# Two groups of recurrences beside the input projection: all tokens' recurrence columns first, split tokens kept in DRAM, RWKV in three groups of PSUM banks, RG-LRU in halves

## The chip, the core and the metric

The kernel runs on one core of a Trainium2 chip. The metric is the device time of one execution in microseconds, as the median of several runs. A core has five engines with their own instruction streams: TensorE (PE: matmuls, with a separate queue of weight loads, PEld), VectorE (DVE), ScalarE (ACT), GpSimd (POOL) and SyncE (SP), which here issues nearly all DMA transfers. Each stream is executed in order. An instruction that needs another engine's result waits, and everything behind it on its engine waits with it.

## The reference

One layer of a hybrid trunk over T = 2048 + 16 tokens of width 1024. The input projection's columns are shared out over three groups of heads; their outputs are joined, projected, and followed by a gated feed-forward network.

```python
p = rms_norm(h, norm_mix_pre[l]) @ w_in[l]
pa = p[..., :A_COLS]
pb = p[..., A_COLS:A_COLS + B_COLS]
pc = p[..., A_COLS + B_COLS:]
oa = rg_lru_group(xa, ya, ...)
ob = forgetting_attention_group(q, k, v, f_logit, ...)
oc, v_own = rwkv7_group(pc, ...)
mixed = jnp.concatenate([oa, ob, oc], axis=-1) @ w_out[l]
h = h + rms_norm(mixed, norm_mix_post[l])
f = causal_dwconv(rms_norm(h, norm_ffn_pre[l]) @ ffn_up[l], ffn_conv[l])
gate, val = jnp.split(f, 2, axis=-1)
f = (jax.nn.gelu(gate, approximate=True) * val) @ ffn_down[l]
h = h + rms_norm(f, norm_ffn_post[l])
```

RG-LRU (256 channels, columns "a", 512 of them) and RWKV-7 (4 heads of 64, columns "c", 1024 of them) are recurrences over the tokens:

```python
_, h = lax.associative_scan(combine, (a, b), axis=1)
...
s_kk = jnp.einsum('bhij,bhj->bhi', S, kk_t)
S = S * w_t[:, :, None, :] - s_kk[..., None] * (kk_t * a_t)[:, :, None, :] + v_t[..., None] * k_t[:, :, None, :]
```

The attention (8 heads of 64, columns q, k, v of 512 each and 8 gate columns) is causal softmax attention with a cumulated forget gate added to the scores.

## The kernel before

All products are float32-like: each operand is split into a high and a low part (`wh`, `wl` of the weights, `xh`, `xl` of the tokens), and `mm3` (L168 to L170) adds three matmuls of the parts.

**Input projection** (`w_in_norm`, `w_in_part`, `w_in_step`). The tokens come in three parts of two blocks each (400 + 384, 384 + 384, 256 + 256 columns). For each part, `w_in_norm` loads, normalises, transposes (tile `pst`) and splits the tokens into `xh` and `xl` in SBUF. Then 24 units of 128 output columns run, in the order c (8 units), a (4), k (4), v (4), q (4); a unit loads 128 columns of `w_in` (tile `raw`, 512 KB), splits them (ACT L162, DVE L163) and makes 8 x 3 matmuls into a bank `psp` for each block. ACT or DVE copies the bank to a staging tile (`stp`, `sth`, `stl`), and SP stores that to DRAM (`scr_p`, `scr_kh`, `scr_kl` and so on). Everything behind the projection reads from DRAM. `psp` has a pool of five PSUM banks; the staging tiles have two slots (`sth`) and one (`stl`, `stv`).

**Recurrences** (`recurrences`, `lru_block`, `Rwkv.block`, `Rwkv.chunks`). They go over nine blocks of four chunks of 64 tokens (the last has one chunk), three blocks for each part of the projection. `lru_block` works on both halves of its 256 channels at once, in buffers that it shares with RWKV (`rwk`, `rwr`, `rwsq`, `rwe`). `Rwkv.block` makes the operands, `chunks` solves a triangular system for each chunk: diagonal blocks go through DRAM (`da`, `rwia`, `dx`, `rwxu`), 15 steps alternate between POOL (L1119) and DVE (L1120), small matmuls follow. Up to the mark `SOLVED` a block is its front; the rest is kept as `R.ending` and put behind the front of the next block. RWKV uses two banks `rps` and one `eps`.

**What sets the order.** The program text runs the projection's units and, through `Beside`, lets the recurrences make `PACE` = 1.5 steps for each unit, once 14 units of the part are out. The framework then schedules all instructions of the program over the engines: each engine's stream is a fixed list that it makes, with an instruction placed where its operands and buffers are planned to be ready. So recurrence rows stand between projection rows on PE, and those that don't fit reach into attention, although the text ends the recurrences first.

**Beside and behind it.** `weight_sums` makes the differences of `ffn_down` (tile `ds`) that the last stage needs: loads, four POOL subtractions for each of ten pairs of rows, stores; its text runs beside the projection. Attention (`Attn.run`) goes over the 8 heads for the first 1024 tokens (score tiles `sc`, maxima `mx`, values `po`; ACT makes the exponentials `p` at L658), then over the 8 heads for the rest, with the output projection (`pswo`) beside it. FFN-up (`ffn_up`, tile `psu`) has three super-blocks of 22 units; in the first one POOL also makes the sums and differences of its weights (`uq`, L1626), DVE and POOL split the operands (`uw`, L1554). FFN-down is tile `psd`.

## Time and profile before

| | us |
|---|---|
| median of 3 runs | 3112.99 (3111.31 to 3129.72) |
| span of the profiled execution | 3106.3 |
| PE busy in the span | 2921.8 (94%) |
| weight load busy | 2493.4 (80%) |
| DVE busy | 2208.1 (71%) |
| ACT busy | 1463.2 (47%) |
| POOL busy | 1318.1 (42%) |

The page gives the profiled execution's span, from its first to its last instruction, and not its total. A matmul's record overlaps with the next one's, since matmuls are pipelined, so PE's busy time is not PE at its peak; the distance from one start to the next is what a matmul takes from the engine. The granted clock is TensorE's, as a share of full speed. By the page's chain of waits, 61% of the span is PE, 14% DVE, 12% DMA.

```profile
PE   6998999999978999999989899999999999999998
PEld 6987988998855664565558899999999999787876
DVE  6248655676688788777745899897778777557766
...
PEclk9999999999977799999999999999999999999999
```

Each column is a fortieth of the span, 78 us. The weight load and the clock fall in the twelfth to fifteenth column, which is where the projection has ended and attention has begun.

### The profile page before, as it was taken

The page shows a single profiled execution, that of the slowest core. Times are in us where ns is not written, and L with a number is a line of the kernel's source. Part 1 is how long each engine was busy: PE and PEld are TensorE (multiplying, and loading weights), DVE is VectorE, ACT ScalarE, POOL GpSimd, SP SyncE. Part 2 cuts the span into 40 slices and gives each one's busy share as a digit, 9 for nine tenths or more (in the row PEclk, how much of TensorE's full clock was granted, in tenths as well). Part 3 has the DMA queues.
Part 4 walks back from the last instruction along what each step waited for, and adds up shares of the span by engine and source line. Part 5 has one row for each costly group of instructions (what it writes and reads, how often), then busy time and mean ns, then how long its engine had stood idle before and what let it go on. Part 6 is the DMA issues. An engine that isn't in the chain of part 4 may idle for free.

```text
span 3106.3 us, 52286 instructions
## 1 busy us (share of the span) xinstructions
PE 2921.8 (94%) x18488; PEld 2493.4 (80%) x18488; DVE 2208.1 (71%) x4322; ACT 1463.2 (47%) x2770; POOL 1318.1 (42%) x1436
## 2 busy tenths in 40 slices
PE   6998999999978999999989899999999999999998
PEld 6987988998855664565558899999999999787876
DVE  6248655676688788777745899897778777557766
ACT  4135334344534444445544555566666665324333
POOL 3310101101133465446743568743533334556665
PEclk9999999999977799999999999999999999999999
DMA  6664333353352334444336455565555565535444
GB/s 202 231 205 142 103 89 107 106 150 98 96 139 65 77 90 128 118 125 107 80 101 199 155 180 167 171 197 169 165 168 163 167 188 160 180 102 173 143 166 143
DMA packets 456502, 443.71 MB, mean 143 GB/s; under 512 B 82496, under 2 KB 373514, under 8 KB 453408
## 3 DMA queue, kind: packets, MB, share of 16 engines
q1 hardware_dynamic: 455856, 439.99, 47.8%
q8 instruction: 145, 2.38, 0.3%
q14 instruction: 117, 0.96, 0.1%
q0 software_dynamic: 384, 0.39, 0.0%
HBM read 314.39 MB, written 125.87 MB: 142 GB/s over the span
## 4 chain that ended last, share of the span: by engine, by line
PE 61%; DVE 14%; DMA 12%; POOL 5%; issue 4%; ACT 3%; SPq 0%; POOLq 0%; DVEq 0%; ACTq 0%
PE psu L168 7%; PE psu L169 7%; PE psu L170 7%; PE psp L168 4%; PE psp L169 4%; PE psp L170 4%; PE po L676 3%; PE psd L170 2%; PE psd L168 2%; PE psd L169 2%; DVE uw L1554 2%; PE mx L527 2%; DVE uy L1665 2%; PE sc L653 2%; PE pswo L170 2%
## 5 line engine op out<-in xcount | busy, mean ns | idle before, releaser
L168 PE MATMUL psu<-xo,uw 128*128 128x344 f32 x1848 | 592.1, 324 | 23.5 <-DVE vb L1709 12.5
L169 PE MATMUL psu<-xo,uw 128*128 128x344 f32 x1848 | 594.5, 322 | 0.0
L170 PE MATMUL psu<-xo,uw 128*128 128x344 f32 x1848 | 584.3, 321 | 0.0
L168 PE MATMUL psp<-xh,wh 128*128 128x384 f32 (+2 forms) x1152 | 380.6, 330 | 0.0
L170 PE MATMUL psp<-xh,wl 128*128 128x384 f32 (+2 forms) x1152 | 377.6, 328 | 3.0 <-DVE wl L163 3.0
L169 PE MATMUL psp<-xl,wh 128*128 128x384 f32 (+2 forms) x1152 | 376.7, 327 | 0.0
L168 PEld LDWEIGHTS psu<-xo,uw 128*128 128x128 f32 x1848 | 348.6, 189 | 28.8 <-DVE vb L1709 15.5
L1554 DVE TENSOR_TENSOR uw<-uq,uw 128x512 fp32r<-128x512 f32 x352 | 333.6, 954 | 53.3 <-ACT uw L1553 49.9
L169 PEld LDWEIGHTS psu<-xo,uw 128*128 128x128 f32 x1848 | 349.8, 189 | 0.0
L170 PEld LDWEIGHTS psu<-xo,uw 128*128 128x128 f32 x1848 | 348.1, 189 | 0.0
L1553 ACT ACTIVATE uw<-uq 128x512 fp32r<-128x512 f32 x462 | 286.9, 627 | 90.9 <-PE psu L170 43.2
L658 ACT ACTIVATE p<-sc,bias 128x512 f32<-128x512 f32 (+4 forms) x352 | 197.5, 591 | 218.9 <-PE sc L654 184.1
L1665 DVE SCALAR_TENSOR_TENSOR uy<-psu,ffn_cols,uy 128x342 f32<-128x342 f32 (+1 forms) x396 | 223.7, 567 | 70.5 <-ACT uy L1663 69.6
L697 POOL TENSOR_TENSOR acc<-acc,p 128x512 f32<-128x512 f32 (+3 forms) x208 | 228.5, 1102 | 84.2 <-DVE acc L697 36.5
L1671 POOL TENSOR_TENSOR uy<-uy,uy 128x342 f32<-128x342 f32 (+1 forms) x132 | 145.8, 1105 | 225.4 <-DVE uy L1665 88.9
L170 PEld LDWEIGHTS psp<-xh,wl 128*128 128x128 f32 x1152 | 218.9, 190 | 10.4 <-issue 5.5
L168 PEld LDWEIGHTS psp<-xh,wh 128*128 128x128 f32 x1152 | 218.8, 190 | 7.1 <-issue 4.7
L169 PEld LDWEIGHTS psp<-xl,wh 128*128 128x128 f32 x1152 | 218.7, 190 | 6.7 <-issue 4.3
L1554 POOL TENSOR_TENSOR uw<-uq,uw 128x512 fp32r<-128x512 f32 x110 | 158.7, 1443 | 137.1 <-ACT uw L1553 116.7
L530 DVE TENSOR_REDUCE mc<-mx 128x1 f32<-128x400 f32 (+5 forms) x320 | 171.8, 554 | 57.5 <-PE mx L527 55.7
L1554 DVE TENSOR_TENSOR fo<-u,fo 128x896 fp32r<-128x896 f32 x88 | 106.4, 1209 | 122.3 <-ACT fo L1553 122.3
L1626 POOL TENSOR_TENSOR uq<-uq,uq 128x512 f32<-128x512 f32 x88 | 137.6, 1566 | 113.0 <-DMA uq<-in_ffn_up_dram 96.4
(460 smaller groups left out, 6539.2 us busy)
## 6 DMA issues: line engine op xcount, KB each, us to landing
uq<-in_ffn_up_dram SPq DMA_DIRECT2D x220, 256.0 KB
uq<-scr_us SPq DMA_DIRECT2D x176, 256.0 KB
raw<-in_w_in_dram SPq DMA_DIRECT2D x72, 512.0 KB
scr_us<-uq SPq DMA_DIRECT2D x88, 256.0 KB
u<-scr_ff SPq DMA_DIRECT2D x88, 256.0 KB
scr_ff<-uy SPq DMA_DIRECT2D x110, 171.0 KB
q<-scr_qh SPq DMA_DIRECT2D x96, 128.0 KB
ds<-in_ffn_down_dram SPq DMA_DIRECT2D x10, 1024.0 KB
```

Of the source, the lines that this page charges most:

```text
L168: nc.tensor.matmul(out, ah, bh, start=first, stop=False, skip_group_check=more)
L169: nc.tensor.matmul(out, ah, bl, start=False, stop=False, skip_group_check=more)
L170: nc.tensor.matmul(out, al, bh, start=False, stop=last, skip_group_check=more)
L530: self.reduced = nc.vector.tensor_reduce(mc[:rows, i, ci : ci + 1], ps[:rows, :full], axis=AX.X, op=ALU.max)
L658: last = nc.scalar.activation(p[:rows, :w], ps[:rows, :w], AF.Exp, bias=bias[:rows, j : j + 1])
L676: mm = nc.tensor.matmul(po[at : at + 64, c0:n], v1[:rows, j], p[:rows, : n - c0], start=start and i < 2, stop=end and i + 2 >= len(group), ...
L697: eng.tensor_tensor(a, ps_[0][0][:rows, c0:n] if start and i == 1 else a, p[:rows, : n - c0], op=ALU.add)
L1553: core.nc.scalar.activation(hi, src, AF.Copy)
L1554: (eng or core.nc.vector).tensor_tensor(lo, src, hi, op=ALU.subtract)
L1626: core.nc.gpsimd.tensor_tensor(raw[:], self.raw[x][:], self.raw[y][:], op=op)
L1665: stt(y[:, :n], src[:, i : n + i], cw[:, 44 * i + cc : 44 * i + cc + 1], y[:, :n], op0=ALU.mult, op1=ALU.add)
L1671: core.pooled = nc.gpsimd.tensor_tensor(v[:, :n], g[:, :n], v[:, :n], op=ALU.mult)
```

## The change

The projection is put in another order, and what lies beside it is fitted into other buffers:

- Four parts instead of three (528, 512, 512, 512 tokens); blocks of 272, 256 and three times 512 columns. The c and a columns of all parts come first, part by part, then k, v and q of parts 2, 3, 0 and 1. The buffers `xh`, `xl` are two sets that take turns, so the split tokens of parts 0 and 1 are stored in DRAM (`scr_xs`) and loaded again. There are 96 loads of weights, not 72.
- Recurrences of a part (two blocks each, three for the last) start when its c and a columns are out, at a pace of 3 steps for each unit. A block runs to its end before the next one's text begins; there is no `SOLVED` and no `ending`.
- PSUM: the projection has three banks, not five; RWKV has two for its solve (`rps`), two for making operands (`eps`) and one for its end (`ops`).
- RG-LRU works on one half of the channels at a time, in buffers of its own; its two halves are put between the steps of RWKV's block.
- Staging tiles of all kinds share three slots. The gate's small tiles move there too.
- The differences of `ffn_down` are made in halves of 256 columns, in FFN-up's text. Attention takes its second bank for maxima from another pool.

```diff
@@ def w_in_norm
+PARTS = 4
+W_IN_TILES = (0, 5, 9, 13, 17)
+W_IN_SPLIT = {0: 3}
...
+    for s, rows in () if kept else tiles:
+        src = meta if s < META else x[s - META : s - META + rows, :]
+        norm_transpose(core, pools, psum, src, rows, gain, [(hi, lo, s - t0, 0, rows)])
+    if part < 2:
+        for i, t in enumerate((hi, lo)):
+            flat = t[:].rearrange("p k t -> p (k t)").bitcast(F32)
+            place = scr["xs"][part, i, :, : KD * n]
+            core.nc.sync.dma_start(*((flat, place) if kept else (place, flat)))
@@ def w_in_step
-        oh = st.tile([P, 400], F32R, tag="sth", name=core.n("sth"))
-        ol = st.tile([P, 400], F32R, tag="stl", name=core.n("stl"), bufs=1)
+        oh = st.tile([P, 512], F32R, tag="sth", name=core.n("sth"))
+        ol = st.tile([P, 512], F32R, tag="sth", name=core.n("stl"))
@@ class WIn
+    def units(self, blocks, columns):
+
+        for kind, c0 in columns:
+            w = w_in_weights(self.core, self.pools, self.w_in, c0)
+            for block in blocks:
+                after = w_in_step(self.core, self.pools, self.psum, w, block, kind, c0, self.scr)
+                self.end()
+                self.waiting = after
+            yield
@@ class Rwkv
+    def po(self):
+
+        return self.epsum.tile([P, 512], F32, tag="ou", name=self.core.n("ops"), bufs=1)
+
     def pe(self):
 
-        return self.epsum.tile([P, 512], F32, tag="ae", name=self.core.n("eps"), bufs=1)
+        return self.epsum.tile([P, 512], F32, tag="ae", name=self.core.n("eps"), bufs=AE)
@@ def lru_block
+        u, r, g, al = (R.t([P, 256], "l" + s)[:, :n] for s in "urga")
...
-    stt(r, r, 1.0, al, op0=ALU.add, op1=ALU.mult)
-    stt(g, g, 1.0, u, op0=ALU.add, op1=ALU.mult)
-    yield
+        stt(r, r, 1.0, al, op0=ALU.add, op1=ALU.mult)
+        stt(g, g, 1.0, u, op0=ALU.add, op1=ALU.mult)
+        yield
@@ def weight_sums
+        for c in (0, 256):
+            t = pool.tile([P, 4, 256], F32, tag="us", name=core.n("ds"), bufs=1)
...
@@ def recurrences
-READY = 13
-PACE = 1.5
+PACE = 3.0
+AHEAD_UNITS = 4
+LRU_AFTER = 0, 1, 3, 4
...
+W_IN_RECUR = (0, 1), (2, 3), (4, 5), (6, 7, 8)
...
+    for b in W_IN_RECUR[part]:
+        lru = lru_block(R.core, R, scr, lk, b)
+        for i, _ in enumerate(R.block(b)):
+            if i in LRU_AFTER:
+                next(lru)
             yield
-        yield from R.ending
-        R.ending = gen
@@ def hybrid_block_kernel
-            ps_mm = pool(p1a, "ps_mm", 5, space=PSUM)
+            ps_mm = pool(p1a, "ps_mm", 5 - AE, space=PSUM)
...
+            for part in (1, 2):
+                units = ca(part)
+                emit(units, AHEAD_UNITS)
+                blocks.append(norm(part + 1))
+                emit(units)
+                gate(part)
+                recur(part)
+            emit(ca(3))
+            gate(3)
+            recur(3)
+            for part in (2, 3, 0, 1):
+                emit(kvq(part))
+                if part > 1:
+                    blocks[part - 2] = norm(part - 2, True)
...
+            if sup == 1 or j == NFF - 1:
+                next(more_sums, None)
```

(AE is 2.) PE's stream before, from the projection's last rows on: `eps` and `rps` are recurrence rows, `sc` and `mx` attention's.

```order
L170 MATMUL psp_9446<-xh_6168,wl_9235 128x256
L1032 MATMUL eps_8749<-rwix_8656,spr 128x256
L1032 MATMUL eps_8752<-rwix_8656,spr 128x256
L1052 MATMUL eps_8779<-rwsq_8649,bones 128x256
L653 MATMUL sc_10919<-q_1481_10828,k_1471_10801 128x512
L653 MATMUL sc_10925<-q_1481_10828,k_1471_10801 128x400
L527 MATMUL mx_10835<-k_1472_10802,q_1474_10806 128x144
L527 MATMUL mx_10840<-k_1472_10802,q_1474_10806 128x272
L527 MATMUL mx_10845<-k_1472_10802,q_1474_10806 128x400
L527 MATMUL mx_10850<-k_1472_10802,q_1474_10806 128x400
L527 MATMUL mx_10853<-k_1472_10802,q_1474_10806 128x128
L1284 MATMUL rps_8288<-ident,rww_895_6444 128x128 x2
```

Recurrence rows go on between attention's here for some 700 rows. PE's stream after, at the last recurrence rows (tile `ops`, of the ninth block):

```order
L168 MATMUL psp_9783<-xh_8502,wh_9746 128x256
L169 MATMUL psp_9783<-xl_8503,wh_9746 128x256
L170 MATMUL psp_9783<-xh_8502,wl_9747 128x256
L1296 MATMUL ops_8495<-ident,rwxu_8457 128x64
L1299 MATMUL ops_8495<-rwsg_8030,g_up 128x64
L168 MATMUL psp_9783<-xh_8502,wh_9746 128x256
L169 MATMUL psp_9783<-xl_8503,wh_9746 128x256
L170 MATMUL psp_9783<-xh_8502,wl_9747 128x256
```

All recurrence rows now stand between projection rows; 21 projection rows of 256 columns and 288 of 512 follow, and then attention's first rows without any recurrence row among them. The first RG-LRU matmul (`ga_w`) has 712 projection matmuls ahead of it before, and 672 now.

POOL's stream before, early in FFN-up's first super-block: `uq` are the sums of its weights, `uw` a split, `uy` products.

```order
L1554 TENSOR_TENSOR uw_17739<-uq_17706,uw_17739 128x512
L1626 TENSOR_TENSOR uq_17961<-uq_17924,uq_17926 128x512
L1626 TENSOR_TENSOR uq_17924<-uq_17922,uq_17924 128x512
L1626 TENSOR_TENSOR uq_17981<-uq_17961,uq_17922 128x512
L1626 TENSOR_TENSOR uq_18001<-uq_17928,uq_17981 128x512
L1554 TENSOR_TENSOR uw_17912<-uq_17767,uw_17912 128x512
L1626 TENSOR_TENSOR uq_18134<-uq_18097,uq_18099 128x512
L1626 TENSOR_TENSOR uq_18097<-uq_18095,uq_18097 128x512
L1671 TENSOR_TENSOR uy_17872<-uy_17849,uy_17872 128x342
```

Only the stage's own rows stand there, and its sums follow each other directly. POOL's stream after, at the same place, with the moved differences (`ds`):

```order
L1576 TENSOR_TENSOR ds_20879<-ds_20879 128x256
L1558 TENSOR_TENSOR uw_17419<-uq_17274,uw_17419 128x512
L1576 TENSOR_TENSOR ds_20879<-ds_20879 128x256 x2
L1632 TENSOR_TENSOR uq_17641<-uq_17604,uq_17606 128x512
L1576 TENSOR_TENSOR ds_20879<-ds_20879 128x256
L1632 TENSOR_TENSOR uq_17604<-uq_17602,uq_17604 128x512
L1677 TENSOR_TENSOR uy_17379<-uy_17356,uy_17379 128x342
L1632 TENSOR_TENSOR uq_17661<-uq_17641,uq_17602 128x512
L1632 TENSOR_TENSOR uq_17681<-uq_17608,uq_17661 128x512
```

The differences now stand between the sums, one or two at a time. All `ds` rows stand within this first super-block.

340 lines of the change are left out of this document (159 added, 181 removed).

## The prediction

> **What bounds the kernel now.** I read the busy time by stage first, then the share of single tiles in it, then the chain of waits. Columns of the windows: PE, PE weight load, VectorE (DVE), ScalarE (ACT), POOL busy, granted clock, DMA share, GB/s.
>
> ```profile
> 0.00:865.00 865.00, 810.58 (x6541) 746.30 (x6541) 522.58 (x1229) 355.31 (x634) 129.14 (x185) 0.98 0.46 138
> 1203.00:1700.00 497.00, 464.40 (x2017) 294.42 (x2018) 353.43 (x774) 238.79 (x444) 271.25 (x281) 0.98 0.46 127
> 1700.00:2640.00 940.00, 912.73 (x5703) 904.03 (x5701) 759.80 (x1145) 565.44 (x1121) 486.60 (x385) 0.99 0.56 169
> 2640.00:3106.00 466.00, 442.22 (x1866) 355.50 (x1866) 299.49 (x360) 164.60 (x273) 283.02 (x354) 0.97 0.45 151
> ...
> 50.00:150.00 100.00, 100.00 (x561) 100.00 (x560) 27.23 (x28) 23.94 (x32) 35.07 (x24) 1.00 0.66 220
> 200.00:865.00 665.00, 646.09 (x5672) 586.24 (x5670) 437.25 (x1010) 298.12 (x542) 59.56 (x116) 0.98 0.40 113
> 865.00:1203.00 338.00, 291.86 (x2364) 193.15 (x2363) 272.82 (x816) 139.07 (x299) 148.09 (x235) 0.79 0.38 92
> 1420.00:1560.00 140.00, 131.86 (x563) 70.22 (x562) 110.20 (x253) 77.39 (x133) 108.54 (x119) 0.99 0.38 90
> ```
>
> Every stage is near PE's limit but one. The projection (to 865 us) keeps PE busy for 810.6 of 865 us. The first half of attention (865 to 1203 us) does not: the weight load is busy for 193 of 338 us, the granted clock is 0.79, and DVE is at 272.8/338 = 0.81, the highest share of any of these stretches. What sits there beside attention are the last recurrences:
>
> ```profile
> L170 PE MATMUL psp<-xh,wl x1152: 274/337/702, 45.2 to 862.6; 128*128 128x384 f32 x95, 128*128 128x256 f32 x64, 128*128 128x400 f32 x33
> L653 PE MATMUL sc<-q,k x352: 170/392/974, 874.5 to 1591.6; 128*128 128x512 f32 x112, 128*128 128x272 f32 x16, 128*16 128x16 f32 x16, 128*128 128x400 f32 x16
> L1143 PE MATMUL rps<-rwxu,rwsc x792: 191/191/238, 367.6 to 1160.6; 32*32 32x32 f32 x198
> ```
>
> The projection's last matmul starts at 862.6, the first score at 874.5, and recurrence matmuls run to 1160.6. The first two windows below are those of the tile `rps`, the last two of `eps` (the recurrences' PSUM tiles): 205.5 us of their PE time lie in the projection, 126.3 us, at the low clock, beside attention.
>
> ```profile
> 0.00:865.00 865.00, 138.50 (x2560) 117.33 (x2560) 66.70 (x137) 33.66 (x67) 0.98 0.46 138
> 865.00:1203.00 338.00, 106.19 (x1602) 87.54 (x1602) 41.04 (x96) 21.35 (x44) 0.79 0.38 92
> ...
> 0.00:865.00 865.00, 66.99 (x219) 30.75 (x219) 22.45 (x58) 26.18 (x56) 0.98 0.46 138
> 865.00:1203.00 338.00, 20.12 (x63) 10.89 (x62) 7.39 (x18) 6.27 (x16) 0.79 0.38 92
> ```
>
> In the new order no recurrence row is left on PE behind the last projection row: the stage from 865 to 1203 loses them, the projection gets them. The sum is what the one saves less what the other pays.
>
> **Wider blocks: 4 us.** Starts of matmuls in a row, 400, 256 and 512 columns wide:
>
> ```profile
> 100.13 0.34 PE L168 MATMUL psp<-xh,wh 128*128 128x400 f32 x1
> ...
> 102.31 0.34 PE L168 MATMUL psp<-xh,wh 128*128 128x400 f32 x1
> ...
> 779.76 0.28 PE L169 MATMUL psp<-xl,wh 128*128 128x256 f32 x1
> ...
> 780.95 0.28 PE L170 MATMUL psp<-xh,wl 128*128 128x256 f32 x1
> ...
> 2699.44 0.39 PE L170 MATMUL psd<-qd,fo 128*128 128x512 f32 x1
> ...
> 2701.06 0.39 PE L168 MATMUL psd<-dw,fo 128*128 128x512 f32 x1
> ```
>
> 12 steps in 2.18 us, 10 in 1.19, 7 in 1.62: 182, 119 and 231 ns. A line through the last two is 7 ns + 0.4375 ns a column (400 give 182). Columns stay the same; matmuls fall from 3456 to 2880 (24 units x 24 x 5 blocks, not 6), 576 x 7 ns = 4 us. The Trainium skill, "TensorE: Matmul & The Clock Gate", section "Wait — 56ns, not 53.3ns?", puts the fixed part of a matmul at about 2.5 ns, which would make it 1.4 us; either way the width is no term that decides.
>
> **Start of the recurrences: 30 us earlier.**
>
> ```profile
> L1377 PEld LDWEIGHTS eps<-rwk,lru_ga_w x36: 186/189/331, 190.1 to 1011.0; 128*128 128x128 f32 x36
> L1018 DVE TENSOR_TENSOR_SCAN rwe<-rst,rwe x9: 403/1225/1457, 223.4 to 1037.5; 128x512 f32<-128x512 f32 x8, 128x128 f32<-128x128 f32 x1
> ```
>
> Ahead of the first RG-LRU matmul (190.1 us) PE had 712 projection matmuls of 400 and 384 columns (127 us by the line); now 672, of which 576 have 272 or 256 columns (93 us), and 16 transposes more (4 us). So about 160 us. The ffn_down differences that lay beside it leave too; I count no gain for that.
>
> **The stretch with recurrences: 745 us.** PE: 1899 projection matmuls lie between the first and the last recurrence row (288 of 272 columns, 267 of 256, 1344 of 512: 378 us). Gate and transposes there I take as half of the two rows below, 22 us, and 7 us for the v columns' transposes.
>
> ```profile
> L139 PE MATMUL pst<-ident,xt 128*128 128x128 f32 (+1 forms) x136 | 24.9, 346 | 25.1 <-DVE xt L126 17.0 <-DVE lruv L1336 7.7 <-DVE rs L90 0.4
> ...
> 0.00:865.00 865.00, 19.30 (x96) 17.47 (x96) 3.00 (x6) 2.70 (x6) 0.98 0.46 138
> ```
>
> The recurrences are 205.5 + 126.3 x 0.79 = 305 us. Sum 712 us; at the share of 200 to 865 us (646/665 = 0.97) 733 us. DVE: 522.6 us of the old stage; plus what the recurrences use of it after 865 us. That is 272.8 less attention's part: 118 steps there, against 109 in the stretch 1420 to 1560 with attention alone (110.2 us), so 119 us, and more for the shorter heads, of which 18 are prepared there against 8 (say 140 to 145). So 130 us. Plus 24 more weight splits at 1.26 us (30), plus RG-LRU in halves: ten operations of 512 become twenty of 256, 2 x 478 less some 740 ns, nine blocks, 19 us.
>
> ```profile
> L658 ACT ACTIVATE p<-sc,bias 128x512 f32<-128x512 f32 (+4 forms) x118 | 60.7, 544 | 82.0 <-PE sc L654 60.3 <-POOL acc L697 9.5 <-PE po L676 6.0
> ...
> L658 ACT ACTIVATE p<-sc,bias 128x512 f32<-128x512 f32 (+4 forms) x109 | 64.1, 619 | 54.1 <-PE sc L654 44.4 <-DVE acc L697 2.7 <-DVE rsv L90 2.4
> ...
> L556 DVE TENSOR_TENSOR q<-mx,ident 4x512 fp32r<-4x512 f32 x18 | 12.3, 682 | 3.2 <-PE mx L545 2.7
> ...
> L556 DVE TENSOR_TENSOR q<-mx,ident 4x512 fp32r<-4x512 f32 x8 | 5.5, 682 | 0.2
> ...
> L163 DVE TENSOR_TENSOR wl<-raw,wh 128x1024 fp32r<-128x1024 f32 x72 | 90.6, 1259 | 14.7 <-ACT wh L162 13.5 <-ACT rwsc L1106 0.9
> L1373 DVE SCALAR_TENSOR_TENSOR rwk<-rwraw,lru_cols,rwk x54: 270/478/631, 182.1 to 981.6; 128x256 f32<-128x256 f32 x42, 128x208 f32<-128x208 f32 x6, 128x64 f32<-128x64 f32 x6
> ```
>
> Together 702 us; off goes what lies ahead of the stretch (522.6 - 437.3 = 85) and behind it (70 us at the 0.27 of 50 to 150 us: 19): 598 us. At the highest share any long stretch shows, 0.81, that is 741 us. So both engines would be at the most they have shown here. I take 745; the ends are 712 (PE never waits) and 840: the blocks' scans stand (1037.5 - 223.4)/8 = 102 us apart, times 8.25 blocks.
>
> **The rest.** Behind the last recurrence row stand 288 matmuls of 512 and 21 of 256 columns: 69 us. The projection ends at 160 + 745 + 69 = 974. The first score follows 12 us later, as now. Then the 118 steps that took until 1203: alone a step took 140/109 = 1.28 us, so 152 us; scaled by DVE's work per step (142/118 against 110/109) 183. I take 174. The point that stood at 1203 comes at 974 + 12 + 174 = 1160: 43 us saved. DMA: 24 more weight loads, four stores and four reloads of the split tokens, all on SP; the reloads are issued one part (over 60 us) ahead of use, behind the stores they could hold up; hidden while the DMA share is 0.40, and at 0.66 (50 to 150 us) PE still was busy all the time. Cost 0.
>
> **ffn_down differences in FFN-up: 6 us lost.** The order puts all 80 halves between POOL's products of the first of three super-blocks (1720 to 2030 us; the second follows).
>
> ```profile
> 1720.00:2030.00 310.00, 289.71 (x1782) 286.06 (x1783) 273.99 (x369) 171.49 (x347) 226.48 (x158) 0.97 0.55 173
> 2030.00:2335.00 305.00, 304.80 (x1941) 303.74 (x1940) 238.68 (x379) 195.63 (x381) 130.17 (x108) 1.00 0.59 172
> ...
> L1572 POOL TENSOR_TENSOR ds<-ds 128x512 f32<-128x512 f32 x40 | 58.3, 1458 | 115.9 <-DMA ds<-in_ffn_down_dram 105.9 <-issue 7.6
> ...
> L1554 DVE TENSOR_TENSOR uw<-uq,uw 128x512 fp32r<-128x512 f32 x110 | 121.8, 1118 | 9.6 <-ACT uw L1553 9.4
> ...
> L1554 DVE TENSOR_TENSOR uw<-uq,uw 128x512 fp32r<-128x512 f32 x113 | 98.3, 875 | 20.0 <-ACT uw L1553 18.5
> ```
>
> POOL goes from 226 to 285 of 310 us: it fits. But the same DVE split takes 1118 ns where POOL is busy for 73%, 875 ns where for 43%; at 92% it gets some 150 ns longer, 17 us over 110, and DVE goes from 274 to 291 of 310. The slack covers it on average; 6 us for the times that it doesn't, 0 to 25 as ends.
>
> Sum: -43 + 6 = -37. The profiled execution has a span of 3106.3 us; its own total is not printed, but the median of the runs, 3113.0, lies 6.7 us above, which I take as what lies around it. 3113 - 37 = 3076 us.
>
> **Rivals.** (1) PE never waits and attention alone goes at its 152 us: 160 + 712 + 69 + 12 + 152 = 1105, 98 us saved, 3015. For it: PE reached 100% from 50 to 150 us. Against: DVE would be at 598/712 = 0.84, above all shown. 17%.
> (2) Banks. Projection tiles have three PSUM banks, not five, and all staging shares three slots. Evacuations wait for the stores of the tile before:
>
> ```profile
> ACT stp L56 <- DMA scr_p<-stp: 59.0, 9, 11.0
> DVE stp L58 <- DMA scr_p<-stp: 58.5, 8, 11.7
> ```
>
> Up to 11.7 us each, hidden today by four spare banks x 24 x 0.175 = 17 us; two spare ones give 11 us, and 6 with blocks of 256. If a quarter to half of the 117 us shows: 3076 + 30 to 59 = 3106 to 3135. 25%.
> (3) A lock. The Trainium skill, "SBUF — State Buffer", section "Who interferes with whom": a VectorE instruction with two SBUF inputs and a GpSimd one that reads SBUF exclude each other, whoever is second waits. The 1118 against 875 ns agree. As a mechanism here: the 58.3 us of differences block DVE for the share that such operations have of its time, at least 121.8/274 = 0.44, 26 us; DVE is at 300 of 310 us, its waits no longer fit, and some 20 us go to PE: 3076 - 6 + 20 = 3090. 10%.
> (4) Slower: the chain of one block. If a block can't follow the last in under the 102 us it takes now (dependent small steps, four trips through DRAM), the stretch is 840 us, PE waits for it in order, 95 us more: 3171. It decides from 745 + 37 = 782 us, or 95 us a block, on; a loss of 1% begins at 98.5. Against: these 102 us come from an order that alternated one block's end with the next one's start at a slower pace. 12%.
>
> **Numbers.** My forecast has 36%, its own range 3050 to 3100. 1% (31 us) is about what a measurement of this kernel can tell from no change. Faster: (1) and mine, 0.53; within 1%: (2) and (3), 0.35; slower: (4), 0.12. The range leaves out the lower half of (1) and most of (4): 3015 to 3140.
>
> **What would show it.** Last projection matmul near 974; first score 12 us later, no recurrence between; last recurrence some 70 us before; granted clock above 0.9 from there to the first w_out matmul; DVE near 0.81 in the stretch with recurrences; first super-block of FFN-up within 10 us of 310. Wrong, if projection evacuations wait for banks or slots with PE idle (2), or PE waits there for recurrence results (4).

## The result, and the profile after

The changed kernel takes 3144.85 us as the median of seven runs (3141.66 to 3152.1), the kernel before 3112.99 (3106.33 to 3133.18); the ratio is 1.0102 (1.0074 to 1.0130). The forecast was 3076 with a range that ended at 3140: the change makes the kernel 1% slower, and the forecast had it faster. The two profiled executions are 39.4 us apart, the medians 31.9, so stages are read to a few microseconds.

The page after has its slices 79 us wide:

```profile
PE   6889899999998888999998889999999999899998
PEld 5767777777896444565567788999999999787776
DVE  4477877776645677667746688797778777547667
...
PEclk9889799999999899999999899999999999999999
```

The dip of the clock that lay in the twelfth to fourteenth column before (7, 7, 7) is gone but for one 8. In its place the first columns have become poor (PE 6, 8, 8; clock 9, 8, 8, 9, 7), and the dip of PE where FFN-up's first super-block lies is wider: 8 in columns 22 to 24 (1651 to 1887 us), where the page before has 8, 9, 8 in columns 21 to 23. Marks of the stages, from the tiles of the changed kernel (first and last start):

```profile
L1007 PE MATMUL eps<-rwwa,wa_up x36: 272/376/480, 159.9 to 793.3; 64*128 64x256 f32 x32, 64*128 64x64 f32 x4
L170 PE MATMUL psp<-xh,wl x960: 277/394/794, 29.3 to 1005.6; 128*128 128x512 f32 x115, 128*128 128x256 f32 x39, 128*128 128x272 f32 x38
L666 PE MATMUL sc<-q,k x352: 170/392/787, 1015.9 to 1602.9; 128*128 128x512 f32 x112, 128*128 128x272 f32 x16, 128*16 128x16 f32 x16, 128*128 128x400 f32 x16
L168 PE MATMUL psu<-xo,uw x1848: 314/321/656, 1705.6 to 2672.3; 128*128 128x344 f32 x185
```

and the one of the kernel before that the prediction did not show:

```profile
L168 PE MATMUL psu<-xo,uw x1848: 314/321/656, 1702.7 to 2633.9; 128*128 128x344 f32 x185
```

The end of FFN-up's first super-block is the start of its 1849th `psu` matmul: 2043.0 before, 2080.7 after. That gives the account (us; the last column is what the prediction's sum amounts to):

| stage | before | after | difference | forecast |
|---|---|---|---|---|
| to the first score | 874.5 | 1015.9 | +141.4 | +111.5 |
| first score to first FFN-up matmul | 828.2 | 689.7 | -138.5 | -154.5 |
| FFN-up, first super-block | 340.3 | 375.1 | +34.8 | +6 |
| the rest | 1063.3 | 1065.0 | +1.7 | 0 |
| span | 3106.3 | 3145.7 | +39.4 | -37 |

Moving the recurrences ahead of attention costs as much as it saves (+141 against -139), and FFN-up's loss is left over. (The +141 already holds a gain: without the differences of `ffn_down` beside it the projection of the kernel before ends 17.7 us earlier, as before_sums shows below.) The same in busy times: windows of the kernel before, then of the changed one, with columns as in the prediction.

```profile
0.00:234.00 234.00, 197.56 (x1049) 189.66 (x1049) 103.37 (x251) 76.60 (x129) 70.20 (x70) 0.98 0.66 212
234.00:865.00 631.00, 613.01 (x5494) 556.64 (x5492) 419.21 (x978) 278.71 (x506) 58.94 (x115) 0.98 0.39 111
...
1703.00:2043.00 340.00, 317.27 (x1941) 311.63 (x1940) 296.34 (x404) 193.10 (x388) 240.17 (x169) 0.97 0.54 170
```

```profile
0.00:234.00 234.00, 172.78 (x1012) 149.61 (x1014) 126.69 (x378) 97.31 (x171) 19.72 (x47) 0.87 0.52 159
234.00:931.00 697.00, 683.44 (x6278) 546.24 (x6278) 507.57 (x1299) 342.54 (x628) 74.35 (x150) 0.96 0.43 121
931.00:1006.00 75.00, 73.26 (x328) 58.11 (x327) 30.84 (x34) 25.60 (x33) 1.84 (x1) 1.00 0.66 207
...
160.00:931.00 771.00, 742.18 (x6523) 590.29 (x6523) 560.31 (x1442) 381.81 (x700) 83.37 (x167) 0.94 0.42 120
160.00:234.00 74.00, 58.74 (x251) 44.06 (x253) 52.74 (x144) 39.27 (x73) 9.02 (x17) 0.79 0.38 105
...
1705.60:2080.70 375.10, 324.50 (x1941) 314.97 (x1940) 297.13 (x403) 192.07 (x386) 308.71 (x249) 0.95 0.66 210
2080.70:2379.60 298.90, 298.19 (x1898) 297.03 (x1897) 230.68 (x372) 189.63 (x370) 127.51 (x107) 1.00 0.55 168
```

Busy time multiplied by the granted clock is a measure of the work that TensorE got done. In the first 234 us it was 197.56 x 0.98 = 194 us before and 172.78 x 0.87 = 150 us after: 43 us less. From 234 us on the two hardly differ: 613.01 x 0.98 / 631 = 0.95 before, (683.44 x 0.96 + 73.26) / 772 = 0.94 after. So the projection lost most of this work at its start, where no recurrence matmul or few of them run, and not in the long stretch in which all recurrences now lie.

### The profile page after: what moved, and what is told of

Same layout as the page of the kernel before. It is cut to its first block, busy times and chain, and to the rows that moved or that the text cites. A ratio compares the mean times of both kernels' runs of the same rounds, so it can differ in the third digit from the quotient of the medians.

```text
span 3145.7 us, 51522 instructions
## 1 busy us (share of the span) xinstructions
PE 2914.4 (93%) x17894; PEld 2399.4 (76%) x17894; DVE 2204.7 (70%) x4432; ACT 1513.0 (48%) x2833; POOL 1313.9 (42%) x1476
## 4 chain that ended last, share of the span: by engine, by line
PE 59%; DVE 13%; DMA 11%; POOL 7%; issue 5%; ACT 3%; SPq 1%; DVEq 0%; POOLq 0%; ACTq 0%
PE psu L168 6%; PE psu L169 6%; PE psu L170 6%; PE psp L170 5%; PE psp L168 4%; PE psp L169 4%; PE po L689 3%; PE pswo L168 2%; PE pswo L169 2%; PE pswo L170 2%; PE mx L540 2%; PE psd L168 2%; PE psd L169 2%; PE psd L170 2%; DMA u<-scr_ff 2%
## 5 line engine op out<-in xcount | busy, mean ns | idle before, releaser
L168 PE MATMUL psp<-xh,wh 128*128 128x512 f32 (+1 forms) x960 | 349.5, 364 | 0.7 <-DVE stp L58 0.4
L170 PE MATMUL psp<-xh,wl 128*128 128x512 f32 (+1 forms) x960 | 347.6, 362 | 1.6 <-DVE wl L163 1.5
L169 PE MATMUL psp<-xl,wh 128*128 128x512 f32 (+1 forms) x960 | 347.5, 362 | 0.0
L710 POOL TENSOR_TENSOR acc<-acc,p 128x512 f32<-128x512 f32 (+3 forms) x208 | 221.5, 1075 | 72.5 <-DVE acc L710 36.1
L543 DVE TENSOR_REDUCE mc<-mx 128x1 f32<-128x512 f32 (+6 forms) x320 | 172.1, 554 | 108.1 <-PE mx L540 104.3
L170 PEld LDWEIGHTS psp<-xh,wl 128*128 128x128 f32 x960 | 184.3, 192 | 32.8 <-DVE wl L163 3.6
L169 PEld LDWEIGHTS psp<-xl,wh 128*128 128x128 f32 x960 | 184.9, 193 | 31.4 <-issue 7.0
L168 PEld LDWEIGHTS psp<-xh,wh 128*128 128x128 f32 x960 | 184.4, 192 | 29.2 <-issue 3.7
L1557 ACT ACTIVATE fo<-u 128x896 fp32r<-128x896 f32 x88 | 81.1, 922 | 210.3 <-POOL u L1787 112.7
```

The lines of the kernel that those rows point to most:

```text
L168: nc.tensor.matmul(out, ah, bh, start=first, stop=False, skip_group_check=more)
L169: nc.tensor.matmul(out, ah, bl, start=False, stop=False, skip_group_check=more)
L170: nc.tensor.matmul(out, al, bh, start=False, stop=last, skip_group_check=more)
L543: self.reduced = nc.vector.tensor_reduce(mc[:rows, i, ci : ci + 1], ps[:rows, :full], axis=AX.X, op=ALU.max)
L710: eng.tensor_tensor(a, ps_[0][0][:rows, c0:n] if start and i == 1 else a, p[:rows, : n - c0], op=ALU.add)
L1557: core.nc.scalar.activation(hi, src, AF.Copy)
```

## The experiments

Each time of a run is given against runs of the kernel before on the same chip (its median there was 3106 to 3112 us), so ratios are compared, not times. Lengths of super-blocks are from the first `psu` matmul to the 1849th, and from there to the 3697th. They come from one profiled execution of each kernel; where the stage is the same they agree to 2 us (375.1 in the changed kernel, 376.3 in before_sums, 374.2 in wl_pool). Kernels of one run have no interval.

### The differences of ffn_down

The text of the changed kernel asks for them in FFN-up's second super-block, but the framework's plan had drawn them all into the first. **sums_second** holds each one back:

```diff
             if sup == 1 or j == NFF - 1:
-                next(more_sums, None)
+                with tc.issue_after(core.pooled.ins):
+                    next(more_sums, None)
```

> The changed kernel, with the differences of ffn_down held back until POOL's product of the unit before, so that they stand in FFN-up's second super-block and not in its first. Theory, the place is what costs: in the first super-block POOL makes sums that ACT, DVE and then PE wait for, in the second it makes none. First super-block 340 us as in the kernel before (375 in the changed one), second at most 5 us longer, time 3108 to 3118. Rival, every difference costs wherever it stands, by its loads and stores or by a lock between POOL and VectorE: what the first super-block gains the second loses, time 3138 to 3146.

**before_sums** is the kernel before with this part of the change alone:

```diff
-            sums = weight_sums(core, pool(p1a, "us", 1), a["ffn_down"], scr)
...
+        more_sums = weight_sums(core, pool(p3, "us", 1, **early), a["ffn_down"], scr)
...
+            if sup == 1 or j == NFF - 1:
+                next(more_sums, None)
```

> The kernel before, with this one part of the change: the differences in halves, in FFN-up's text, not beside the projection. Theory, the differences alone make FFN-up's loss: first super-block 370 to 380 us, projection the same or up to 10 us shorter, time 3135 to 3150. Rival, something else in the changed kernel makes it: first super-block 340 to 348 us, time 3103 to 3120.

**no_subs** and **subs_only** part the work from the traffic:

```diff
-            sub(l0, r0, l0)
-            sub(r0, r1, r0)
-            sub(r1, r1, l0)
-            sub(l1, l1, r1)
```

> The changed kernel without POOL's subtractions: the differences' tiles are stored as they were loaded, so the four subtractions of each half are left out while all loads and stores stay in the first super-block. Theory, POOL's queue is what costs: first super-block 338 to 346 us. Rival, the traffic of the loads and stores costs: 360 to 375 us. A split between the two would show as a value between.

```diff
+    t = pool.tile([P, 4, 256], F32, tag="us", name=core.n("ds"), bufs=1)
+    for i in range(2):
+        nc.sync.dma_start(t[:, 2 * i : 2 * i + 2], ...)
     for k in range(DOWN_PAIRS):
         for c in (0, 256):
-            t = pool.tile([P, 4, 256], F32, tag="us", name=core.n("ds"), bufs=1)
-            for i in range(2):
-                nc.sync.dma_start(...)
...
```

> The changed kernel, with POOL's 80 subtractions of the differences in the first super-block, but on one tile that is loaded once; the other loads are left out, and the stores stand in the third super-block. no_subs, with loads and stores alone, took 362.7 us there against 375.1 with both and 340.3 with neither. If the two add up, subtractions alone take 350 to 355 us. If they only cost together (POOL waiting for its data late in its order), they take 341 to 347 us. If POOL is what costs and the traffic only hides the rest, 365 us or more.

**sums_actq** and **sums_poolq** issue the same loads and stores from another engine (`nc.scalar` or `nc.gpsimd` for `nc.sync`):

> The changed kernel, with the loads and stores of the differences issued by ACT and not by SP. Theory, most of the 35 us in FFN-up's first super-block is SP's queue: it stands for the differences' single buffer (15 us for scr_ds, 16 us for POOL) with FFN-up's own loads behind. With them on ACT the first super-block takes 345 to 358 us. Rival, bandwidth and POOL's time cost, whoever issues: 370 us or more (more still if ACT now stands in SP's place).

> The same with POOL as the issuer, whose stores then wait for nothing that is not done on POOL itself. Theory of SP's queue: 345 to 360 us for the first super-block. Rival, bandwidth and POOL's time: 370 us or more.

Measured:

| kernel | ratio to before (95%) | first super-block | second |
|---|---|---|---|
| before | | 340.3 | 298.2 |
| changed | 1.0102 (1.0074 to 1.0130) | 375.1 | 298.9 |
| sums_second | 1.0052 (1.0033 to 1.0071) | 342.8 | 313.8 |
| before_sums | 1.0060 (1.0034 to 1.0087) | 376.3 | 297.4 |
| no_subs | one run, 3138.1 | 362.7 | 298.5 |
| subs_only | one run, 3146.6 | 372.4 | 296.4 |
| sums_actq | one run, 3139.2 | 377.0 | 297.6 |
| sums_poolq | one run, 3163.7 | 382.1 | 317.5 |

before_sums shows the loss without anything else of the change: its first super-block is 36 us longer. Its projection, free of the differences, ended 17.7 us earlier (844.9 for 862.6), and the sum is 0.6% slower than before. Held back to the second super-block the differences cost 15.6 us there, between my two theories: the place matters, and they are not free elsewhere.

Why the first super-block pays is told by what VectorE waits for in it. The waits of DVE in that window, of the kernel before:

```profile
DVE xt L1515 <- DMA xt<-scr_h: 14.0, 4, 5.3
DVE uw L1554 <- ACT uw L1553: 9.9, 15, 3.2
```

of the changed kernel:

```profile
DVE xt L1519 <- DMA xt<-scr_h: 29.6, 6, 12.8
DVE uw L1558 <- ACT uw L1557: 27.3, 18, 4.5
```

The window's DVE column above says 296 of 340 us: VectorE had 44 us to spare before, and it takes its instructions in order. With the differences these two waits grow from 23.9 to 56.9 us, by 33, and the super-block by 34.8.

Which of the two belongs to what, no_subs and subs_only tell, if they are read up to the same point. The text of subs_only puts the stores into the third super-block, but in its trace all 20 stand in the first, at 1939 to 1974 us, right behind the last subtraction (1938 us). So I compare the waits from the first `psu` matmul to the 1009th, which started after 201.8 us in the kernel before. Up to there no_subs has all its loads and stores but the last one and no subtraction, subs_only all 80 subtractions, two loads and no store. The kernel before:

```profile
DVE xt L1515 <- DMA xt<-scr_h: 14.0, 4, 5.3
DVE uw L1554 <- ACT uw L1553: 2.2, 5, 0.8
```

no_subs (traffic alone), 13 us behind the kernel before at this matmul:

```profile
DVE xt L1519 <- DMA xt<-scr_h: 32.0, 6, 12.6
DVE uw L1558 <- ACT uw L1557: 2.7, 4, 1.2
```

and subs_only (subtractions alone), 21 us behind:

```profile
DVE xt L1519 <- DMA xt<-scr_h: 18.7, 6, 5.6
DVE uw L1558 <- ACT uw L1557: 11.8, 3, 6.4
```

The traffic makes the loads of `scr_h` late. The subtractions make POOL's sums (`uq`) late, for which ACT's and then VectorE's split `uw` waits: ACT's waits for these sums are 10.0 us in the whole super-block before, 36.0 in the changed kernel. Behind the split in VectorE's order stands the evacuation of a `psu` bank, for which PE waits. PE's waits in the whole super-block, of the kernel before and then of the changed one:

```profile
PE psu L168 <- DVE vb L1709: 12.1, 7, 3.8
PE psu L168 <- ACT vb L1701: 1.1, 1, 1.1
```

```profile
PE psu L168 <- DVE vb L1715: 25.6, 7, 10.7
PE psu L168 <- ACT vb L1707: 8.1, 8, 1.6
```

All of PE's waits there grow from 22.5 to 50.5 us, by 28; PE is busy 7 us longer, at a clock of 0.95 for 0.97. So each cause costs by itself, and the 10 to 15 us that I had thought likely for the subtractions (350 to 355 us for the super-block) were too few. Whether the two add up is open: behind that matmul no_subs lost another 9 us, although its last store was issued at 1928 us, and subs_only, with its stores, another 11. No run explains this late part. SP's queue is not needed for the loss of the subtractions, since subs_only had next to nothing in it up to there. With ACT as issuer the super-block took 377 us, with POOL 382, and there the differences reached into the second; but both only put the transfers into another busy queue.

The split itself did not get longer on average (window of the first super-block, before and then changed kernel):

```profile
L1554 DVE TENSOR_TENSOR uw<-uq,uw 128x512 fp32r<-128x512 f32 x133 | 142.3, 1081 | 10.1 <-ACT uw L1553 9.9
```

```profile
L1558 DVE TENSOR_TENSOR uw<-uq,uw 128x512 fp32r<-128x512 f32 x133 | 141.8, 1077 | 27.8 <-ACT uw L1557 27.3
```

### The projection's start

**consts_own** gives the tiles of the recurrences' constants buffers of their own:

```diff
-    rows = pool.tile([P, 512], F32, tag="sth", name=core.n("rows"))[:, :P]
+    rows = pool.tile([P, P], F32, tag="colrows", name=core.n("rows"), bufs=1)
...
-    v = pool.tile([P, 512], F32, tag="sth", name="lruv")[:, :12].rearrange("p (a b) -> p a b", b=2)
+    v = pool.tile([P, 6, 2], F32, tag="lruv", name="lruv", bufs=1)
```

> The changed kernel, with the tiles of the recurrences' constants in small buffers of their own and not in the three staging slots. Theory, the shared slots hold the constants back, ACT stands at them, and the second part's tokens wait behind on ACT (PE is idle for some 30 us of 64 to 95 us): constants out by 30 us, the last projection matmul 10 to 18 us earlier than 1005.6, time 3127 to 3135. Rival, the second part's tokens are late anyway, their loads standing behind stores on SP: projection's end within 4 us of 1005.6, time 3141 to 3147.

**norm_ahead** does so too, and normalises parts 2 and 3 earlier in the text:

```diff
             gate(0)
+            blocks.append(norm(2))
             recur(0)
...
-                units = ca(part)
-                emit(units, AHEAD_UNITS)
-                blocks.append(norm(part + 1))
-                emit(units)
+                emit(ca(part))
                 gate(part)
+                if part == 1:
+                    blocks.append(norm(3))
                 recur(part)
```

> The changed kernel, with the constants in own buffers as in consts_own, and with the tokens of parts 2 and 3 normalised as soon as the columns c and a and the gate of the part two before are done, in the text ahead of that part's recurrences and not four units into the next part. Theory, the hand-over from part to part is what the start lost: PE waits at transposes of tokens that VectorE reaches behind gate and recurrence work (26 us of the 139 to 234 us are lost, clock 0.81). The stretch up to the first rps matmul gets 12 to 20 us shorter, the projection's end goes from 1005.6 to 982 to 992, time 3120 to 3132 against 3113 before (on the same chip: 12 to 24 us less than the changed kernel). Rival, what is won at the hand-over is lost again by recurrences that start later: projection's end within 6 us of that of consts_own (1000.0).

**k_early** gives PE more work at the first two hand-overs:

```diff
             recur(0)
+            emit(win.units(blocks[0], KVQ[:4]))
...
                 recur(part)
+                if part == 1:
+                    emit(win.units(blocks[1], KVQ[:4]))
...
-                emit(kvq(part))
+                emit(kvq(part) if part > 1 else win.units(blocks[part], KVQ[4:]))
```

> The changed kernel, with the k columns of parts 0 and 1 made directly behind their columns c and a, not near the projection's end. Theory, PE is starved at the start because c and a of one part last it only some 30 us, less than the next part's tokens need: with 20 us more work at each of the first two hand-overs the projection loses 10 to 25 us less, last projection matmul at 981 to 996 (1005.6), time 12 to 25 us less than the changed kernel. Rival, the start is bound by the recurrences' chain or by the work of VectorE as a whole: projection's end within 6 us of 1005.6, or later because the recurrences now reach to its end.

The last projection matmul started at 1000.0, 1002.0 and 1002.6 (1005.6 in the changed kernel); the ratios are 1.0106 (1.0078 to 1.0135), 1.0100 (1.0073 to 1.0127) and 1.0179 (1.0160 to 1.0197). All three of my theories fell. The first 234 us of each (one window of each kernel, in the order above):

```profile
0.00:234.00 234.00, 176.35 (x1022) 152.19 (x1023) 127.86 (x377) 98.08 (x171) 17.81 (x47) 0.85 0.52 161
```

```profile
0.00:234.00 234.00, 172.06 (x1102) 149.52 (x1103) 134.99 (x390) 103.14 (x183) 19.28 (x48) 0.89 0.53 165
```

```profile
0.00:234.00 234.00, 169.74 (x1105) 151.65 (x1106) 135.01 (x398) 103.71 (x185) 23.38 (x47) 0.86 0.54 166
```

Busy time multiplied by clock is 150, 153 and 146 us, as in the changed kernel (150) and not as before (194): the waits moved, and the start stayed as it was. k_early in addition has its recurrences end late (their last matmul at 996 for 931), and FFN-up began 13 us later (1718.6 for 1705.6); why, these runs don't tell.

**four_banks** (`AE = 1` for 2) tested the banks of my second rival:

> The changed kernel with four PSUM banks for the projection and one for the operands of RWKV (three and two in the changed one). My rival of the prediction, banks: evacuations wait for banks, the projection gets 10 to 30 us shorter. Against it, that PE waited for no evacuation: projection's end within 8 us of 1005.6, or later, because the operands now wait for their one bank.

One run took 3291.1 us. The projection's last matmul started at 894.4, but the recurrences, with one bank for their operands, went on to 1148 beside nothing else:

```profile
894.00:1148.00 254.00, 187.20 (x1688) 144.06 (x1687) 143.00 (x434) 85.34 (x176) 31.46 (x61) 0.52 0.08 21
```

The second bank for operands is worth some 145 us in this order. The run takes a bank from the operands as it gives one to the projection, so it says nothing for or against three banks there; in the changed kernel PE's waits name an evacuation once before 234 us, for 0.4 us, and none from there to 1006 us.

**wl_pool** moves 72 of 96 weight splits from VectorE to POOL:

```diff
...
+    split(core, hi[:], lo[:], raw[:], core.nc.gpsimd)
```

> The changed kernel, with the low part of w_in's weights from the 25th unit on (72 of 96) made by POOL and not by VectorE. Three edits at the projection's start moved its waits and not its end (1000 to 1006 us), so what bounds is still open. Theory, VectorE: it loses 72 x 1.24 = 89 us of its 570 in the stretch with recurrences, its queue reaches the next tokens and the recurrences' operands sooner, and the stretch gets 15 to 50 us shorter: last projection matmul at 955 to 990, time 15 to 50 us less than the changed kernel. Rival, PE itself with its small matmuls (busy for 0.96 of the stretch) bounds: projection's end within 8 us of 1005.6. Third, POOL is slower and weights come later, or shuts VectorE out: end later than 1010.

The ratio is 1.0280 (1.0245 to 1.0315), the projection ended at 1065.7. This is the third case, worse than I had put it, and it doesn't isolate VectorE: POOL's split took 2.5 us, and in 234 to 990 us POOL stood 220 us in all for ACT's copies of the weights, with the recurrences' POOL steps behind it in its order. **lean_lru** takes work from VectorE and gives it to nobody:

```diff
-        for i in range(3):
-            stt(u, raw[:, i : n + i], ...)
...
-        nc.vector.tensor_tensor_scan(u, al, g, k["h"][:, pc], op0=ALU.mult, op1=ALU.add)
```

> The changed kernel with RG-LRU's work on VectorE left out (17 operations of each half block, some 130 us in all, and 6 of ScalarE's), while its loads, matmuls and store stay: TensorE's work is the same to the matmul. Theory, VectorE and the steps that wait for it set the length of the stretch with recurrences: projection's end at 950 to 985. Rival, TensorE with its small matmuls sets it: end within 8 us of 1005.6.

Its last projection matmul stood at 994.0, and DVE was busy for 576.5 us up to there (665.1 in the changed kernel): 89 us less work of VectorE, not the 130 that I had put, gave 12. (The run also leaves out seven operations of ScalarE and one of the two loads in each half block.) That lies between my two theories (the rival's 8 us end at 997.6) and nearer to the rival: in this one run VectorE's work set little of the stretch's length. **no_recurrences** leaves both recurrences out:

```diff
-            recur = lambda part: beside.add(recurrences(R, lk, scr, part))
+            recur = lambda part: None
...
```

> The changed kernel with both recurrences left out (zeros stand in their rows): the projection alone, in the new order. Its matmuls, transposes and gates are some 600 us of starts. If the hand-over of tokens from part to part is lost by itself, as in the first 139 us (43 us lost there with no recurrence yet), the projection ends at 660 to 690; if the recurrences make the later losses, at 640 to 655. The difference to 1005.6, against the recurrences' 279 us of matmul starts, is what they cost the projection.

**no_rec_slots** is the same with six slots for three in the two pools `nt` (rows of x and raw weights) and `st` (staging):

> no_recurrences (both recurrences left out, zeros in their rows) with six slots each, not three, for staging and for the buffers that x's rows and w_in's weights share; there is room for them only without the recurrences. Without recurrences TensorE did as little in the first 234 us (busy for 164.5 us at clock 0.89) as with them (172.8 at 0.87), so the start's loss belongs to the projection's own new order. Theory, slots: the next part's rows wait for a buffer; with twice as many TensorE is busy for 185 us or more of the first 234, and the last projection matmul comes 15 to 40 us earlier than 704.5. Rival, the chain of one row tile (load, square, scale, transpose, split) and the traffic: within 8 us of 704.5.

The projection's matmuls and the first 234 us, of no_recurrences (two views):

```profile
L170 PE MATMUL psp<-xh,wl x960: 277/394/795, 43.1 to 704.5; 128*128 128x512 f32 x115, 128*128 128x256 f32 x39, 128*128 128x272 f32 x38
```

```profile
0.00:234.00 234.00, 164.52 (x963) 145.57 (x964) 104.44 (x287) 78.18 (x117) 8.88 (x26) 0.89 0.59 190
```

and of no_rec_slots:

```profile
L170 PE MATMUL psp<-xh,wl x960: 276/388/796, 28.3 to 667.4; 128*128 128x512 f32 x115, 128*128 128x256 f32 x39, 128*128 128x272 f32 x38
```

```profile
0.00:234.00 234.00, 187.54 (x1068) 165.79 (x1069) 100.56 (x289) 78.33 (x120) 8.87 (x26) 0.91 0.59 188
```

Without any recurrence the start is about as poor as with them: 164.52 x 0.89 = 146 us of work in 234, where the changed kernel has 150. The last projection matmul, at 704.5, came later than either of my ranges. Some 14 us of that are the experiment's own, since the tile of zeros holds one of the three slots at first (the first matmul of this row stands at 43.1 us for 29.3 in the changed kernel). From the first to the last matmul the rows give 661.4 us with three slots and 639.1 with six: 22 us belong to slots. Not all of them are the start's: in the first 200 us behind the first matmul (from 43 and from 28 us) TensorE got 163.52 x 0.87 = 142 and 171.84 x 0.89 = 153 us of work done, so 11 of the 22 lie there, a quarter of the 43. Which of the two pools it is, these runs don't tell, and with the recurrences there was no room to try six slots. With three slots or six, with recurrences or without, PE waits at the start for the transposes' operands and for the gate (PE's waits of the changed kernel, 120 to 235 us):

```profile
PE pst L139 <- DVE xt L126: 8.5, 3, 5.0
PE eps L407 <- DVE gc L395: 6.1, 1, 6.1
```

The transposes of the next part's rows stand in PE's order and wait for them. Their waits make 45 us in all in the changed kernel's first 235 us, and 25 before: 20 of the 25 us by which PE is less busy there; the lower clock (0.87 for 0.98) is the rest of the 43. A part lasts PE longer than the 30 us of k_early's theory: its columns c and a are 288 matmuls of 512 columns (576 narrower ones in part 0), 67 us at 231 ns. But only some of them stand ahead of the next part's transposes: 288 of 272 and 256 columns, 35 us, ahead of part 1's, and 384 more, 57 us, between those and part 2's. These two stretches took 64 and 112 us (28.7 to 92.8 and on to 204.8). In each the follower has four 128-row tiles to load, square, scale and split.

### Attention

**hold_first** holds the output projection of the first two rows:

```diff
-                with tc.issue_after(at.steps[-2].ins) if i in HELD else nullcontext():
+                with tc.issue_after(at.steps[-2 if i in HELD else 17].ins) if i in HELD or not i else nullcontext():
```

> The changed kernel, with the output projection of its first two rows held until the first step of attention's second half has ended, as rows 7 and 8 are held already. Theory, attention's second half loses some 15 us because ACT stands 12 us for those rows' mixed values (1187 to 1199 us) and then all 48 matmuls of them go in one piece: the output projection starts some 20 us later, FFN-up 6 to 12 us earlier than 1705.6. Rival, the wait only moves, since these matmuls have to be made anyway and PE had the work: FFN-up's start within 4 us of 1705.6.

In the changed kernel ACT stands at those rows, and PE behind it (ACT's and PE's timeline):

```profile
1199.34 0.22 ACT L162 ACTIVATE mh<-raw 128x16 fp32r<-128x16 f32 x1 [12.03 <-DMA raw<-scr_mix]
```

```profile
1199.61 0.59 PE L168 MATMUL pswo<-woh,mh 128*2 128x512 f32 x1 [4.10 <-ACT mh L162]
```

Held, the output projection began at 1257.8 instead of 1199.6, ACT waited 11.7 us for the same data there, and FFN-up began at 1709.0 instead of 1705.6; the ratio is 1.0108 (1.0065 to 1.0151). The rival holds: the wait only moves. So what attention lost against the forecast stays open.

### Two cures together, and the kernel before without the differences

> k_early together with sums_second: if both gains are independent, 15 us (sums_second) and what k_early gives add up, time 3105 to 3118 against 3113 before. If the projection does not gain from k_early, about 3125.

1.0115 (1.0100 to 1.0131) against 1.0179 for k_early: 20 us for holding the differences back, against 15 in sums_second: that cure works in either order of the projection.

> wl_pool together with sums_second. If the two are independent: what wl_pool gives against the changed kernel and 15 us more. Faster than the kernel before only if wl_pool gives over 17 us.

1.0218 (1.0183 to 1.0253) against 1.0280: 19 us, again about the same.

> The kernel before, with the differences moved out of the projection (which made it 17.6 us shorter in before_sums) and held back to FFN-up's second super-block (where they cost 15.6 us in sums_second, against 35 in the first). If both carry over: 1 to 5 us less than the kernel before, not to be told from no change. Rival, the gain in the projection was chance or is lost in attention: 10 to 16 us more.

1.0006 (0.9990 to 1.0022). The projection ended 14 us earlier (848.5), the second super-block took 318 us, 20 more: no change, as expected. No version that I ran beats the kernel before.

## Why the prediction was wrong

The forecast's -37 us became +39 in the profiled executions, 76 us off. Three terms of its sum failed, and none alone turns the sign: the projection came out 30 us too late, attention alone saved 16 us less, and FFN-up lost 29 us more; the rest is 2.

- **The stretch with recurrences, 745 us, was mis-sized.** By the rows above it took 771 (159.9 to 931), with 742.18 x 0.94 = 698 us of work where I had counted 712. The work was right to 2%. I turned it into time by shares that hold for the middle of a long stage, PE's of 200 to 865 us (0.97, 733 us) and VectorE's (0.81, 741 us), and left out that the new order's start is poorer: the row 160 to 234 us has PE at 58.74 of 74 us and the clock at 0.79, so 28 of the 74 us were lost there. This is 26 of the 76 us, the tail with 75 for 69 another 6.
- **Its cause was a rival's, in another place.** My second rival said slots and banks, through evacuations that wait for stores. Banks fell (of PE's waits only 0.4 us are for an evacuation). Slots hold in part: 22 us without recurrences, 11 of them at the start; that they act through the rows of the next part, and act so beside the recurrences, is argued from PE's waits and not shown. That the pool of these rows went from four buffers to three stood in the change, and I gave it no price.
- **Start of the recurrences** at 159.9 us, as forecast (160), though the first RG-LRU matmul, which I had counted to, came at 171.3 behind RWKV's; that the two errors met was luck.
- **The chain of one block (rival 4, slower) fell.** The scans of two blocks are 78.6 us apart, (795.7 - 166.9) / 8, far under the 95 at which it decides. The kernel did get slower, but not by this:

```profile
L1029 DVE TENSOR_TENSOR_SCAN rwe<-rst,rwe x9: 717/1214/1226, 166.9 to 795.7; 128x512 f32<-128x512 bf16 x8, 128x128 f32<-128x128 bf16 x1
```

- **VectorE at 0.81** did not come: 560.31 of 771 us is 0.73, and lean_lru shows that VectorE set little of the length. Nor was 0.81 the highest share on view, as rival 1 was told: the prediction's row of 1720 to 2030 us has VectorE at 273.99 of 310, 0.88.
- **Attention alone, -154 us, was 16 us too much.** The clock went up, from 0.79 to 0.89 (1016 to 1200 us), a little less than the 0.9 that I had named. My mark was step 118 of the exponentials, and in the kernel before the output projection's first 48 matmuls lie behind it and in the changed one ahead, so the mark compared different work; it came at 1227 (forecast 1160). The stretch from the first score to FFN-up's first matmul, which has the same work in both but for the recurrences, took 689.7 us where the sum implied 673.7. hold_first did not get any of these 16 us back, so their cause stays open. (The step scaled by VectorE's work comes to 181 us, not 183; it changes nothing here.)
- **FFN-up, 6 us, should have been 35, and this is the term whose mechanism I had wrong.** I asked whether POOL and VectorE fit into 310 us on average (285 and 291). They fitted, though POOL got 68.5 us more to do and not 58. (The 310 us were a window; the super-block itself has 340.3 before.) But VectorE's 17 us of longer splits never came, and what came was 33 us of waiting in order, for sums and for loads. The end that I had put at 25 was too low, and of this part's gain, 17.7 us in the projection of before_sums, I said that I counted none. Alone it makes the kernel 0.6% slower, by the point values more than half of the whole loss; by subtraction some 13 us are left for all else, with intervals of about 9 us on either number.
- **The lock (rival 3) is there, but its price fell.** The split took 1081 ns on average before and 1077 after, with POOL busy for 240 and 309 us, and VectorE's busy time did not grow (296 and 297 us). Taken one by one, though, the splits of this super-block follow POOL: those that began while no POOL instruction ran took 674 to 694 ns in both kernels (38 of 133 before, 21 after), and those that began while one ran took 1242 ns on average before (95 of them) and 1151 after (112). With the differences more splits met POOL and took less each, which fits the differences' shorter instructions on POOL (1.0 us for 256 columns, 1.5 us for a sum of 512). So the two super-blocks' 1118 and 875 ns were read rightly; what failed was to let the mean grow with POOL's busy time.

Still open: three quarters of the start's 43 us, why the waits move but stay under three different orders, and attention's 16 us.

## What to carry to other kernels

Work that moves from a poorly used stage into a well used one only pays if the engine gets the work done there at the old rate: multiply busy time by granted clock, and look at the hand-overs, where buffers that were cut to make room are first missed. An engine that is busy for 87% of a stage and takes its work in order had no slack to give here: 33 us more of two waits for operands came out as 35 us of time, although every engine fitted on average. Text that asks for work in one place is no proof that it stands there: look at the order, and hold it back if the place matters. And a mean that stays the same is no proof that a mechanism is absent: split the group by what ran beside each instruction.

## What the runs showed of the hardware

VectorE and POOL made each other wait, instruction by instruction. Four rows of the kernel before, in FFN-up's second super-block (start and duration in us):

```profile
2105.96 1.30 POOL L1554 TENSOR_TENSOR uw<-uq,uw 128x512 fp32r<-128x512 f32 x1
2106.09 1.71 DVE L1554 TENSOR_TENSOR uw<-uq,uw 128x512 fp32r<-128x512 f32 x1
2108.21 0.68 DVE L1554 TENSOR_TENSOR uw<-uq,uw 128x512 fp32r<-128x512 f32 x1
2108.52 1.15 POOL L1671 TENSOR_TENSOR uy<-uy,uy 128x342 f32<-128x342 f32 x1 [1.26 <-DVE uy L1665]
```

The first split of VectorE began 0.13 us behind one of POOL and ended 0.54 us after it; the second began with POOL idle and took 0.68 us, although POOL began within it. VectorE's products that have one operand in PSUM show nothing of this (L1706, `psu` from `psu` and `u`): all 66 took 508 to 525 ns. In wl_pool, where POOL makes splits of 1024 columns, it takes a single instruction to raise a group's mean:

```profile
776.19 2.91 POOL L1566 TENSOR_TENSOR wl<-raw,wh 128x1024 fp32r<-128x1024 f32 x1 [2.32 <-ACT wh L1565]
777.38 1.99 DVE L76 SCALAR_TENSOR_TENSOR rwbk<-rwbk 4x256 f32<-4x256 f32 x1
```

The same operation takes 407 ns with POOL idle; this one alone puts the mean of its 24 from 386 ns in the changed kernel to 452. The Trainium skill, "SBUF — State Buffer", section "Who interferes with whom", has a VectorE instruction with two SBUF inputs and a GpSimd one that reads SBUF exclude each other. These rows agree with it. And in four_banks, where only recurrences were left to PE, its granted clock was 0.52 though it was busy for 187 of 254 us: in that stretch short matmuls with waits between them did not bring the clock up.
